# Phase one of a hybrid encoder layer: two buffers for the convolved tile, and the leading products of a block's first feature tile put ahead of those with the tokens' rest

## The chip, the core and the metric

The kernel runs on one core of a Trainium2 chip. The core has five engines with queues of their own: TensorE (PE, with weight loads shown apart as PEld), VectorE (DVE), ScalarE (ACT), GpSimd (POOL) and SyncE (SP, which here issues the DMAs). An engine executes its instructions in the order in which they stand; semaphores make it wait for the others. The metric is the device time of one execution in microseconds (us); 0.3% of it is 8.8 us.

## What is computed

One inference step of one layer for 2048 prompt frames and 32 sample frames of width 1024. The parts of the reference that phase one covers:

```python
h = rmsnorm(x, p['g_mix_pre'])
proj = h @ p['w_in']               # q, k, v (512 each), z (512), xbc (768), dt (8)
xbc_c = silu(causal_dwconv(xbc, conv_prev, w, b))   # 4 taps in time
xh, bm, cm = split(xbc_c)          # 512 + 128 + 128 features
y, h_fin = ssd_scan(xh, dt, a, bm, cm, h0)
y = rmsnorm((y + d_skip * xh) * silu(z), p['g_ssm_out'])
```

After it come stick-breaking attention over q, k, v, the output projection, and a gated feed-forward part with a convolution of width 3, each with its norms and residuals. All inputs and outputs are float32. A float32 product is made of three faster ones: weights and tokens are each split into a leading part (`hi`, type fp32r) and a rest (`lo`), and `hi*hi + hi*lo + lo*hi` is summed in PSUM.

## The kernel before, in words

The 2080 tokens go through phase one in four blocks (`SBS`): three of 512 and one of 544, which carries the sample's 32 and whose groups are cut into two tiles of 272. `phase_in` builds the blocks one after the other (lines 355 to 613), and a scheduler at build time orders the instructions of each engine by their dependencies and estimated lengths, so work of neighbouring blocks is mixed. For a block s:

- `split` (line 314) makes the tokens' leading parts `xhi` on ACT (L319) and the rests `xlo` on DVE (L320), eight 128-feature slices (k-chunks) each. Their pool has one buffer, so a slice can be written only when TensorE has used the same slice of the last block. Block 0 has a form of its own, `first` (L334, L335).
- `dense` (line 158) makes one output tile of 128 features in a PSUM bank named `o`, of which there are two: 24 matmuls, all at L161. For each k-chunk they are `whi*xhi`, `whi*xlo`, `wlo*xhi`.
- Six feature tiles of xbc, in the order 4, 5, 0, 1, 2, 3 (line 371). For each, ACT copies the bank into `raw` (L377), DVE does the first tap (L384) and three more (L388) into `xc`, ACT takes a sigmoid of it (L392), DVE multiplies (L393). `xc` has one buffer. Weights are loaded by SP, split by ACT (L145) and POOL (L146).
- V: eight groups of 24 matmuls of 260 columns (L412), through the same two `o` banks; ACT copies each out into `v` (L421).
- The SSD scan (lines 476 to 565) on DVE, ACT and TensorE, with TensorE filled up by the K and Q groups (L161 again); it works on `xc` in place. Its DMAs (acB, eA) go through SP.
- `prep` (line 295) loads the next block's tokens, sums their squares on ACT (L306) and POOL (L307), and scales them by the root on DVE (L310, eight instructions).
- `gate` (line 616): four groups for z (L161); ACT takes a sigmoid (L627), DVE multiplies with the bank (L628, for block 0 after L625), which sets the bank free, and then `xc` (L630).
- `gate_norm` (line 637): squares (L641, L644, L645), a root (L177, L180, L183), the scaling of `xc` in place (L650), its split on ACT (L654) and POOL (L656, the last readers of `xc`), and the DMAs out (L657, L658).

With one buffer, the next block's first L384 has to come after the last block's L656.

Of the kernel before, what the change touches and what calls it, by code (L numbers as in the profile page):

```python
# [8 lines left out]
F32 = mybir.dt.float32  # L9
# [22 lines left out]
P = 128  # L32
# [33 lines left out]
def tiles_of(n):  # L66
    return [(0, n)] if n <= 512 else [(0, n // 2), (n // 2, n)]


class Kernel:  # L70
# [81 lines left out]
    def parts(self):  # L152
        return tuple([self.xp.tile([P, 544], F32R, name=f"{e}{k}") for k in range(KC)] for e in ("xhi", "xlo"))

    def dense(self, ps, w, x, c0, c1, k0=0, first=True, last=True, pin=False, loose=False):
        nc = self.nc
        xhi, xlo = x
        for k, (whi, wlo) in enumerate(w):
            hi, lo = xhi[k0 + k][:, c0:c1], xlo[k0 + k][:, c0:c1]
            for i, (l, r) in enumerate(((whi, hi), (whi, lo), (wlo, hi))):  # L160
                mm = nc.tensor.matmul(  # L161
                    ps[:, : c1 - c0], l, r,
                    start=first and i == 0 and k == 0,
                    stop=last and i == 2 and k == len(w) - 1,
                    **({"skip_group_check": True} if loose else {}),
                )
                if pin and i == 0 and k == 0:
                    self.pin(mm)
        if pin:
            self.mark(mm)  # L170

# [81 lines left out]
def phase_in(kn, ctx):  # L253
    nc, tc, a, o = kn.nc, kn.tc, kn.a, kn.o
# [60 lines left out]
    def split(s, x):  # L315
        nt = SBS[s][1]
        xhi, xlo = kn.parts()
        for k in range(KC):
            nc.scalar.copy(xhi[k][:, :nt], x[:, k, :nt])  # L319
            nc.vector.tensor_tensor(  # L320
                xlo[k][:, :nt], x[:, k, :nt], xhi[k][:, :nt].bitcast(F32), op=ALU.subtract
            )
        return xhi, xlo

    def first():

        nt = SBS[0][1]
        x = ep.tile([P, KC, 544], F32, name="x")
        xhi, xlo = kn.parts()
        sq = tmp.tile([P, 544], F32, name="sq", bufs=1)  # L330
        for k in range(KC):
            if k % 2 == 0:
                nc.sync.dma_start(x[:, k : k + 2, :nt], a["xT"][:, k : k + 2, :nt])
            nc.scalar.activation(xhi[k][:, :nt], x[:, k, :nt], AF.Copy, scale=kn.col(C_GMIX + k))  # L334
            nc.vector.scalar_tensor_tensor(  # L335
                xlo[k][:, :nt], x[:, k, :nt], kn.col(C_GMIX + k), xhi[k][:, :nt].bitcast(F32),
                op0=ALU.mult, op1=ALU.subtract,
            )
        for k in range(KC):
            if k == 0:  # L340
                nc.scalar.activation(sq[:, :nt], x[:, k, :nt], AF.Square)
            else:
                t = tmp.tile([P, 550], F32, name="t")
                nc.scalar.activation(t[:, :nt], x[:, k, :nt], AF.Square)
                nc.vector.tensor_tensor(sq[:, :nt], sq[:, :nt], t[:, :nt], op=ALU.add)
        return (xhi, xlo), kn.rstd_narrow(rp, psm, "st", [sq], nt, D, tag="r0")
# [8 lines left out]
    for s, (t0, nt) in enumerate(SBS):  # L355
        last = s == NSB - 1
        if s == 0:
            xs, r0 = first()
            rcol = kn.rcol
        else:  # L360
            xs = split(s, nxt)
        xhi, xlo = xs
        raw = ep.tile([P, 6, 550], F32, name="raw")
        xc = kn.xcp.tile([P, 6, 547], F32, name="xc")
        W = 547 if last else 512
        nc.vector.tensor_copy(raw[:, :, 0:3], hist[:])
        if last:
# [3 lines left out]
        for c in (4, 5, 0, 1, 2, 3):  # L371
            w = wfirst if s == 0 and c == 4 else kn.weight(wp, a["wbx"][c])
            for c0, c1 in tiles_of(nt):
                ps = psd.tile([P, 512], F32, name="o")
                kn.dense(ps, w, xs, c0, c1)
                e = min(c1, 512)
                nc.scalar.copy(raw[:, c, 3 + c0 : 3 + e], ps[:, : e - c0])  # L377
                if c1 > 512:
                    nc.scalar.copy(raw[:, c, 518:550], ps[:, e - c0 : c1 - c0])
            if s == 0:  # L380
                nc.vector.tensor_tensor(raw[:, c, 3 : 3 + nt], raw[:, c, 3 : 3 + nt], r0[:, :nt], op=ALU.mult)
            y = xc[:, c, :W]
            wc = C_SW + c * 4
            nc.vector.tensor_scalar(  # L384
                y, raw[:, c, 0:W], kn.col(wc), kn.col(C_SB + c), op0=ALU.mult, op1=ALU.add
            )
            for i in range(1, 4):
                nc.vector.scalar_tensor_tensor(  # L388
                    y, raw[:, c, i : i + W], kn.col(wc + i), y, op0=ALU.mult, op1=ALU.add
                )  # L390
            t = tmp.tile([P, 550], F32, name="t")
            nc.scalar.activation(t[:, :W], y, AF.Sigmoid)  # L392
            nc.vector.tensor_tensor(y, y, t[:, :W], op=ALU.mult)  # L393
# [12 lines left out]
        for b in range(nb):  # L406
            q = min(P, nt - b * P)
            vp = [psd.tile([P, 512], F32, name="o") for _ in range(2)]
            for h in range(2):
                for k in range(KC):  # L410
                    for i, (l, rr) in enumerate(((xhi, wv[0]), (xlo, wv[0]), (xhi, wv[1]))):
                        nc.tensor.matmul(  # L412
                            vp[h][:q, :260], l[k][:, b * P : b * P + q], rr[:, k, h * 260 : h * 260 + 260],
                            start=i == 0 and k == 0, stop=i == 2 and k == KC - 1,
# [40 lines left out]
        ps = psm.tile([P, 512], F32, name="st")  # L455
# [10 lines left out]
        ps = psm.tile([P, 512], F32, name="st")  # L466
# [6 lines left out]
        for b in range(nb):  # L473
# [22 lines left out]
            for g in range(2):  # L496
                rows = slice(g * 64, g * 64 + 64)
                nc.tensor.matmul(cy[:q, g, :q], xc[rows, 4, sl], xc[rows, 5, sl], start=True, stop=True)
                for i in range(2):
# [3 lines left out]
                        start=True, stop=True,  # L503
# [15 lines left out]
            ps = psm.tile([P, 512], F32, name="st")  # L519
# [11 lines left out]
            ps = psm.tile([P, 512], F32, name="st")  # L531
# [16 lines left out]
            ps = psm.tile([P, 512], F32, name="st")  # L548
# [24 lines left out]
        for name, dst in (("wk", kn.kS), ("wq", kn.qS)):  # L573
            for c in range(4):
                w = kn.weight(wp, a[name][c])
                hi = so.tile([P, 544], F32, name="khi")[:].bitcast(F32R)
                lo = so.tile([P, 544], F32, name="klo")[:].bitcast(F32R)
                kf = so.tile([P, 544], F32, name="kf")
                for c0, c1 in tiles_of(nt):
                    ps = psd.tile([P, 512], F32, name="o")  # L580
# [20 lines left out]
        bufs = {"khi": 2, "klo": 2, "t": 2, "sq": 1}  # L601
# [870 lines left out]
def build(nc, tc, a, o):  # L1472
    kn = Kernel(nc, tc, a, o)
    with ExitStack() as ctx:
# [17 lines left out]
        with ExitStack() as c2:  # L1492
            kn.wp, kn.unit, kn.wbufs, kn.rbufs = c2.enter_context(tc.tile_pool(name="weights_in", bufs=1)), KC, 2, 2
            rest = phase_in(kn, c2)
# [125 lines left out]
```

## Time and profile before

| | us |
|---|---|
| median of 3 runs | 2937.35 |
| the runs, lowest to highest | 2936.06 to 2943.05 |
| the profiled execution, its own time | 2941.02 |
| its span in the profile | 2939.2 |
| TensorE busy | 2814.1 (96%) |
| VectorE, ScalarE, GpSimd busy | 1690.8, 1263.4, 1275.4 |

Phase one lies between 0 and about 650 us of the span. In the timeline each row gives the start, the length, the engine, the line and the tiles written and read, `xN` for merged neighbours, and in brackets the time that the engine sat idle before it and what ended that. The waits view sums these idle times by waiting and awaited line: total, times, longest. In the windows view there is, for a stretch, the busy time of an engine and the clock that TensorE was granted (1.00 is full).

### The profile page before, as it was taken

The numbers are of one execution on the slowest core, as the hardware profiler recorded it, in microseconds if no ns is written. First come the engines' busy times: TensorE is split into PE (matmuls) and PEld (weight loads), VectorE is DVE, ScalarE is ACT, GpSimd is POOL, SyncE is SP. The second block draws the span as 40 slices with busy tenths as digits, with TensorE's granted clock in tenths as the row PEclk, the third lists the DMA queues.
The fourth block names the chain that finished last, engine by engine and source line by source line (L and its number), as shares of the span: only waits on it lengthen the run. The fifth ranks groups of instructions, "written<-read, shape, count | busy, mean of one in ns | idle before, by whom it ended". The sixth has DMA issues, their size and how long they took to land.

```text
span 2939.2 us, 46252 instructions
## 1 busy us (share of the span) xinstructions
PE 2814.1 (96%) x16771; PEld 2427.5 (83%) x16771; DVE 1690.8 (58%) x2628; ACT 1263.4 (43%) x2622; POOL 1275.4 (43%) x1131
## 2 busy tenths in 40 slices
PE   7999999989889999999999999999999999999997
PEld 6777777977788888897788888977888889999997
DVE  7667586566773555447555556675666653623333
ACT  4344444337665555446333444654444443321111
POOL 4565555435766666656322323453223233511113
PEclk9999999989999999999999999999999999999999
DMA  5646464648787778777655556656555445765556
GB/s 179 183 137 193 132 176 124 174 115 271 247 282 263 253 263 276 266 256 250 215 180 172 174 180 219 225 182 205 176 172 170 160 159 202 241 181 179 170 178 200
DMA packets 333093, 586.47 MB, mean 200 GB/s; under 512 B 73306, under 2 KB 192738, under 8 KB 332866
## 3 DMA queue, kind: packets, MB, share of 16 engines
q1 hardware_dynamic: 332866, 583.52, 62.1%
q8 instruction: 134, 2.20, 0.3%
q14 instruction: 93, 0.76, 0.1%
HBM read 445.70 MB, written 137.69 MB: 198 GB/s over the span
## 4 chain that ended last, share of the span: by engine, by line
PE 72%; DVE 13%; DMA 7%; ACT 3%; issue 2%; POOL 1%; SPq 1%; DVEq 0%; ACTq 0%; POOLq 0%
PE o L161 35%; PE u L161 12%; PE t L161 10%; PE z L863 4%; PE pa L904 4%; PE pt L882 3%; DVE xc L388 2%; DMA acB<-acD 2%; PE o L412 1%; DVE acB L488 1%; DVE prow L714 1%; DMA xr<-hS 1%; DVE xc L384 1%; DVE xlo L320 1%; DVE x L310 1%
## 5 line engine op out<-in xcount | busy, mean ns | idle before, releaser
L161 PE MATMUL o<-xhi,w 128*128 128x512 f32 (+2 forms) x3968 | 1047.9, 346 | 24.1 <-ACT xhi L334 8.0
L161 PEld LDWEIGHTS o<-xhi,w 128*128 128x128 f32 x3968 | 697.3, 191 | 119.0 <-ACT xhi L334 8.0
L161 PE MATMUL o<-xlo,w 128*128 128x512 f32 (+2 forms) x1984 | 683.8, 345 | 6.3 <-DVE xlo L320 4.2
L146 POOL TENSOR_TENSOR w<-wraw,w 128x512 fp32r<-128x512 f32 (+3 forms) x244 | 384.3, 1577 | 261.4 <-ACT w L145 232.2
L719 POOL TENSOR_TENSOR beta<-beta,prow 128x512 f32<-128x512 f32 (+3 forms) x256 | 252.5, 987 | 442.7 <-DVE prow L714 366.8
L161 PEld LDWEIGHTS o<-xlo,w 128*128 128x128 f32 x1984 | 380.0, 192 | 50.4 <-DVE xlo L320 6.1
L161 PE MATMUL u<-xhi,w 128*128 128x512 f32 x1056 | 350.3, 398 | 0.0
L161 PE MATMUL o<-ah,w 128*128 128x512 f32 x992 | 344.4, 403 | 4.3 <-DVE f L1348 3.8
L1300 POOL TENSOR_TENSOR y<-y,gb 128x512 f32<-128x512 f32 (+1 forms) x88 | 116.0, 1318 | 503.2 <-ACT gb L1299 503.1
L714 DVE TENSOR_TENSOR_SCAN prow<-gam,prow,z 128x513 f32<-128x513 f32 x192 | 245.2, 1278 | 74.1 <-ACT beta L712 69.7
L887 DVE TENSOR_TENSOR wt<-pt,wt 128x512 fp32r<-128x512 f32 (+2 forms) x320 | 191.0, 602 | 159.6 <-ACT wt L886 157.8
L886 ACT CAST wt<-pt 128x512 fp32r<-128x512 f32 (+2 forms) x320 | 166.9, 527 | 218.2 <-PE pt L882 216.3
L145 ACT CAST w<-wraw 128x512 fp32r<-128x512 f32 (+3 forms) x244 | 172.1, 705 | 170.6 <-PE o L161 98.6
L161 PEld LDWEIGHTS u<-xhi,w 128*128 128x128 f32 x1056 | 199.1, 189 | 46.8
L161 PEld LDWEIGHTS o<-ah,w 128*128 128x128 f32 x992 | 187.2, 189 | 47.0 <-DVE f L1348 6.0
L711 ACT ACTIVATE gam<-z 128x512 f32<-128x512 f32 (+2 forms) x320 | 172.3, 538 | 96.0 <-PE z L863 53.9
L161 PE MATMUL u<-xlo,w 128*128 128x512 f32 x528 | 209.5, 397 | 0.0
L161 PE MATMUL o<-al,w 128*128 128x512 f32 x496 | 196.7, 397 | 0.0
L161 PE MATMUL t<-xhi,w 128*128 128x272 f32 x960 | 189.6, 293 | 2.6 <-DMA w<-wS_up 1.7
L882 PE MATMUL pt<-ident,beta 128*128 128x128 f32 x1088 | 180.3, 277 | 4.2 <-DVE wt L887 2.7
L1292 DVE SCALAR_TENSOR_TENSOR y<-gb,cv,y 128x512 f32<-128x512 f32 (+1 forms) x176 | 142.4, 809 | 72.6 <-ACT y L1290 69.9
L904 PE MATMUL pa<-wt,v 128*64 128x256 f32 (+3 forms) x1152 | 172.3, 280 | 8.6 <-DVE wt L887 6.6
(275 smaller groups left out, 4956.4 us busy)
## 6 DMA issues: line engine op xcount, KB each, us to landing
w<-wS_up SPq DMA_DIRECT2D x264, 512.0 KB, 3.6
w<-wS_dn SPq DMA_DIRECT2D x144, 384.0 KB, 3.5
wS_up<-w SPq DMA_DIRECT2D x88, 512.0 KB, 3.4
w<-wS_out SPq DMA_DIRECT2D x78, 512.0 KB, 5.7
wraw<-wup SPq DMA_DIRECT2D x88, 256.0 KB, 4.0
k<-kS SPq DMA_DIRECT2D x80, 256.0 KB, 4.1
v<-vS SPq DMA_DIRECT2D x80, 256.0 KB, 3.8
wS_dn<-w SPq DMA_DIRECT2D x48, 384.0 KB, 3.1
```

The source lines that it names most:

```text
L145: nc.scalar.copy(hi, raw[:, :m, :])
L146: nc.gpsimd.tensor_tensor(lo, raw[:, :m, :], hi.bitcast(F32), op=ALU.subtract)
L161: mm = nc.tensor.matmul(ps[:, : c1 - c0], l, r, start=first and i == 0 and k == 0, stop=last and i == 2 and k == len(w) - 1, **({"skip_gro ...
L711: nc.scalar.activation(g[:, c0:512], z, AF.Sigmoid, scale=-0.125)
L714: nc.vector.tensor_tensor_scan(back(pr), back(g), z[:, 0:1].to_broadcast([P, n + 1]), self.kn.ones[:, 0:1] if prev is None else prev, op0= ...
L719: eng.tensor_tensor(b[:, :n], b[:, :n], pr[:, c0 + 1 : 513], op=ALU.mult)
L863: mm = nc.tensor.matmul(z[:, :n], q[:, P * b : P * b + P], k[:, :n], start=e == 0, stop=e == 1 and kc < s)
L882: mm = nc.tensor.transpose(t[:, P * j : P * j + P], w[:, P * j : P * j + P], kn.ident[:])
L886: nc.scalar.copy(hi, t)
L887: nc.vector.tensor_tensor(lo, t, hi.bitcast(F32), op=ALU.subtract)
L904: nc.tensor.matmul(av[:m, 2 * P * p + c0 : 2 * P * p + 2 * P], v[:, j, :m], wt[:, rest, j, c0:], start=kc == s and p + j + rest == 0, stop ...
L1292: nc.vector.scalar_tensor_tensor(y[:, :W], gb[:, i : i + W], kn.col(wc + i), y[:, :W], op0=ALU.mult, op1=ALU.add)
```

## The change

`xc` gets two buffers. `dense` gets a switch `rests`: with it the 16 products with the leading part of the tokens come first and the 8 with the rests last; it is set for the first feature tile (c == 4) of each block. The sums and their number are the same.

```diff
-    def dense(self, ps, w, x, c0, c1, k0=0, first=True, last=True, pin=False, loose=False):
+    def dense(self, ps, w, x, c0, c1, k0=0, first=True, last=True, pin=False, loose=False, rests=False):
         nc = self.nc
         xhi, xlo = x
+        terms, late = [], []
         for k, (whi, wlo) in enumerate(w):
             hi, lo = xhi[k0 + k][:, c0:c1], xlo[k0 + k][:, c0:c1]
-            for i, (l, r) in enumerate(((whi, hi), (whi, lo), (wlo, hi))):
-                mm = nc.tensor.matmul(
...
+            terms += [(whi, hi), (wlo, hi)] if rests else [(whi, hi), (whi, lo), (wlo, hi)]
+            late += [(whi, lo)] if rests else []
+        for i, (l, r) in enumerate(terms + late):
+            mm = nc.tensor.matmul(
+                ps[:, : c1 - c0], l, r,
+                start=first and i == 0,
+                stop=last and i == 3 * len(w) - 1,
...
-        xc = kn.xcp.tile([P, 6, 547], F32, name="xc")
+        xc = kn.xcp.tile([P, 6, 547], F32, name="xc", bufs=2)
...
-                kn.dense(ps, w, xs, c0, c1)
+                kn.dense(ps, w, xs, c0, c1, rests=c == 4)
```

Every line from 172 of the kernel before on stands three lines lower in the changed one (L384 is L387 there). The scheduler moves other work with it. Three places in the order of instructions:

VectorE, where block 1 follows block 0; `xc_236` is block 0's tile, `xc_1601` block 1's, `t_1638` the sigmoid of block 1's first feature tile, `rstd2` block 0's root. Before:

```order
L320 TENSOR_TENSOR xlo7_1583<-x_1005,xhi7_1575 128x512
L628 TENSOR_TENSOR t_1518<-t_1519,t_1518 128x512
L630 TENSOR_TENSOR xc_236<-xc_236,t_1518 128x512
L183 RECIPROCAL rstd2_1535<-rstd2_1535 128x512
L650 SCALAR_TENSOR_TENSOR xc_236<-xc_236,cv_63,rstd2_1535 128x512 x4
L384 TENSOR_SCALAR xc_1601<-raw_1600,cv_63 128x512 x5
L388 SCALAR_TENSOR_TENSOR xc_1601<-raw_1600,cv_63,xc_1601 128x512 x7
```

The same place in the changed kernel:

```order
L633 TENSOR_TENSOR xc_236<-xc_236,t_1518 128x512
L387 TENSOR_SCALAR xc_1601<-raw_1600,cv_63 128x512
L391 SCALAR_TENSOR_TENSOR xc_1601<-raw_1600,cv_63,xc_1601 128x512 x3
L396 TENSOR_TENSOR xc_1601<-xc_1601,t_1638 128x512
L387 TENSOR_SCALAR xc_1601<-raw_1600,cv_63 128x512
L391 SCALAR_TENSOR_TENSOR xc_1601<-raw_1600,cv_63,xc_1601 128x512 x3
L396 TENSOR_TENSOR xc_1601<-xc_1601,t_1676 128x512
L186 RECIPROCAL rstd2_1535<-rstd2_1535 128x512
L387 TENSOR_SCALAR xc_1601<-raw_1600,cv_63 128x512
L653 SCALAR_TENSOR_TENSOR xc_236<-xc_236,cv_63,rstd2_1535 128x512 x4
L391 SCALAR_TENSOR_TENSOR xc_1601<-raw_1600,cv_63,xc_1601 128x512
```

Two feature tiles of block 1 are now convolved ahead of block 0's root, and the others right behind it.

ScalarE in block 2, where V begins; `t_2978` to `t_3168` are the six sigmoids of the block in order, `o_3173` the first V bank, `o_3174` the second. Before:

```order
L421 COPY v_3223<-o_3173 128x260
L421 COPY v_3223<-o_3174 128x260
L392 ACT_TABLE_LOAD
L392 ACTIVATE t_2978<-xc_2941 128x512
L392 ACTIVATE t_3016<-xc_2941 128x512
L421 COPY v_3283<-o_3233 128x260
L421 COPY v_3283<-o_3234 128x260
L392 ACTIVATE t_3054<-xc_2941 128x512
L392 ACTIVATE t_3092<-xc_2941 128x512
L421 COPY v_3343<-o_3293 128x260
```

The same place in the changed kernel (`o_3100` and `o_3138` are the banks of feature tiles 2 and 3):

```order
L395 ACTIVATE t_3054<-xc_2941 128x512
L395 ACTIVATE t_3092<-xc_2941 128x512
L380 COPY raw_2940<-o_3100 128x512
L145 CAST w_3751<-wraw_3749 128x1024
L395 ACTIVATE t_3130<-xc_2941 128x512
L380 COPY raw_2940<-o_3138 128x512
L145 CAST w_3792<-wraw_3790 128x1024
L424 COPY v_3223<-o_3173 128x260
L395 ACTIVATE t_3168<-xc_2941 128x512
L309 ACTIVATE t_3700<-x_3693 128x544
L309 ACTIVATE t_3703<-x_3693 128x544
L424 COPY v_3223<-o_3174 128x260
```

All six sigmoids stood behind the first two V copies. Five now stand ahead of the first V copy, and three of these (`t_3054`, `t_3092`, `t_3130`) ahead of the copies of feature tiles 2 or 3.

VectorE, where block 2 follows block 1; `t_2758` and `t_2792` belong to the first two gate groups, `x_2353` is block 2's input. Before:

```order
L213 MEMSET rn_v_3727 128x8
L310 SCALAR_TENSOR_TENSOR x_2353<-x_2353,cv_63,rstd_2390 128x512 x8
L628 TENSOR_TENSOR t_2758<-o_2733,t_2758 128x512
L628 TENSOR_TENSOR t_2792<-o_2767,t_2792 128x512
L630 TENSOR_TENSOR xc_1601<-xc_1601,t_2758 128x512
```

The same place in the changed kernel:

```order
L631 TENSOR_TENSOR t_2758<-o_2733,t_2758 128x512
L633 TENSOR_TENSOR xc_1601<-xc_1601,t_2758 128x512
L216 MEMSET rn_v_3727 128x8
L313 SCALAR_TENSOR_TENSOR x_2353<-x_2353,cv_63,rstd_2390 128x512 x8
L631 TENSOR_TENSOR t_2792<-o_2767,t_2792 128x512
```

The first gate product has moved ahead of the eight scalings. On ScalarE the copy of the root that the scalings wait for (L251 there) has moved behind that product's sigmoid and a square that reads its result.

More of the change, by code (lines that the diff above doesn't have):

```diff
@@ L153, in parts @@
         return tuple([self.xp.tile([P, 544], F32R, name=f"{e}{k}") for k in range(KC)] for e in ("xhi", "xlo"))
-    def dense(self, ps, w, x, c0, c1, k0=0, first=True, last=True, pin=False, loose=False):
+    def dense(self, ps, w, x, c0, c1, k0=0, first=True, last=True, pin=False, loose=False, rests=False):
         nc = self.nc
         xhi, xlo = x
+        terms, late = [], []
         for k, (whi, wlo) in enumerate(w):
             hi, lo = xhi[k0 + k][:, c0:c1], xlo[k0 + k][:, c0:c1]
-            for i, (l, r) in enumerate(((whi, hi), (whi, lo), (wlo, hi))):
[L161 to L168, printed above, removed]
+            terms += [(whi, hi), (wlo, hi)] if rests else [(whi, hi), (whi, lo), (wlo, hi)]
[5 more added lines that the diff above has]
+                stop=last and i == 3 * len(w) - 1,
+                **({"skip_group_check": True} if loose else {}),
+            )
+            if pin and i == 0:
+                self.pin(mm)
         if pin:
```

## The prediction

> **What bounds the kernel now.** I read the engines' busy times first, then the windows of 100 us, then TensorE's waits in phase one and their places in the timeline. The first row is from the page; the others are stretches in us with PE's busy share, then all PE busy time (number of matmuls), granted clock, DMA share and GB/s.
>
> ```profile
> PE 2814.1 (96%) x16771; PEld 2427.5 (83%) x16771; DVE 1690.8 (58%) x2628; ACT 1263.4 (43%) x2622; POOL 1275.4 (43%) x1131
> ...
> 600.00:700.00 100.00, 87.68 (x652) 0.91 0.59 179
> 700.00:800.00 100.00, 86.97 (x625) 0.93 0.73 241
> 800.00:900.00 100.00, 92.57 (x628) 0.98 0.80 279
> ```
>
> TensorE is the bound; VectorE, the next, has 58%. Its instructions keep their number, so the change can only fill its idle time or raise its clock. Outside phase one it is idle mainly in 600 to 900: 12.3 + 13.0 + 7.4 = 32.8 us. The waits view of PE from 0 to 660 (total, times, longest) shows what the change can reach:
>
> ```profile
> PE o L412 <- ACT v L421: 8.9, 3, 3.4
> PE o L161 <- DVE t L628: 5.1, 2, 2.6
> PE o L161 <- DVE xlo L320: 4.2, 3, 1.8
> ```
>
> These 18.2 us are the ceiling for waits. The timeline gives their places, each with its idle time in brackets:
>
> ```profile
> 179.34 0.50 PE L161 MATMUL o<-xlo,w 128*128 128x512 f32 x1 [1.63 <-DVE xlo L320]
> 224.95 0.39 PE L412 MATMUL o<-wvhi,xhi 128*128 128x260 f32 x1 [2.88 <-ACT v L421]
> 318.59 0.48 PE L161 MATMUL o<-xhi,w 128*128 128x512 f32 x1 [2.64 <-DVE t L628]
> 337.85 0.50 PE L161 MATMUL o<-xlo,w 128*128 128x512 f32 x1 [1.81 <-DVE xlo L320]
> 386.07 0.39 PE L412 MATMUL o<-wvhi,xhi 128*128 128x260 f32 x1 [3.43 <-ACT v L421]
> 484.04 0.47 PE L161 MATMUL o<-xhi,w 128*128 128x512 f32 x1 [2.48 <-DVE t L628]
> 544.76 0.58 PE L412 MATMUL o<-wvhi,xhi 128*128 128x260 f32 x1 [2.58 <-ACT v L421]
> ```
>
> **The buffer: V's waits.** Here is why ACT copies V late; the first row is from the view of the tile xc (its engine idle in all, times), then ACT and DVE.
>
> ```profile
>   POOL klo L656: 18.4, 3
> ...
> 377.35 1.28 ACT L392 ACT_TABLE_LOAD   x1
> 384.46 1.29 ACT L392 ACTIVATE t<-xc 128x512 f32<-128x512 f32 x2 [5.83 <-DVE xc L388]
> 385.66 0.63 ACT L421 COPY v<-o 128x260 f32<-128x260 f32 x2
> ...
> 207.49 4.44 DVE L384 TENSOR_SCALAR xc<-raw,cv 128x512 f32<-128x512 f32 x5 [5.64 <-POOL klo L656]
> ```
>
> VectorE waits 18.4 us at three boundaries for POOL to read the old `xc`; the convolution comes late; ACT reaches a sigmoid 5.83 us before its input is there, and the V copies queued behind it hold both banks (3.43 us of PE at 386.07). The order of the changed kernel removes it at the root: two feature tiles are convolved ahead of the old block's scaling and the others follow it without a wait for POOL. So the 8.9 us go.
>
> A wait is added in their place: the sigmoids now stand ahead of the raw copies of feature tiles 2 and 3. Behind these copies on ACT stand V's, and PE needs the bank of feature tile 3 when its second V group begins. For block 1, the rows before are:
>
> ```profile
> 193.83 3.35 DVE L183 RECIPROCAL rstd<-rstd 128x512 f32<-128x512 f32 x1 [11.42 <-ACT rstd L180]
> 197.22 4.63 DVE L650 SCALAR_TENSOR_TENSOR xc<-xc,cv,rstd 128x512 f32<-128x512 f32 x4
> ...
> 210.66 0.59 ACT L377 COPY raw<-o 128x512 f32<-128x512 f32 x1 [4.11 <-PE o L161]
> 213.53 0.38 ACT L421 COPY v<-o 128x260 f32<-128x260 f32 x1 [1.33 <-PE o L412]
> ...
> L388 DVE SCALAR_TENSOR_TENSOR xc<-raw,cv,xc x72: 736/744/2920, 42.7 to 542.9; 128x512 f32<-128x512 f32 x54, 128x547 f32<-128x547 f32 x18
> L384 DVE TENSOR_SCALAR xc<-raw,cv x24: 532/540/2645, 38.1 to 534.7; 128x512 f32<-128x512 f32 x18, 128x547 f32<-128x547 f32 x6
> L392 ACT ACTIVATE t<-xc x24: 629/632/667, 51.8 to 543.8; 128x512 f32<-128x512 f32 x18, 128x547 f32<-128x547 f32 x6
> L393 DVE TENSOR_TENSOR xc<-xc,t x24: 678/686/1814, 54.3 to 544.5; 128x512 f32<-128x512 f32 x18, 128x547 f32<-128x547 f32 x6
> ...
> L388 DVE SCALAR_TENSOR_TENSOR xc<-raw,cv,xc 128x512 f32<-128x512 f32 (+1 forms) x72 | 62.8, 922 | 0.0
> L384 DVE TENSOR_SCALAR xc<-raw,cv 128x512 f32<-128x512 f32 (+1 forms) x24 | 24.8, 1075 | 18.4 <-POOL klo L656 18.4
> ```
>
> The last raw copy now stands behind the fifth sigmoid. If the root comes when it did, it ends at 197.2; one first tap (0.54) and the four scalings (4.63) end at 202.4. Then come nine taps of 0.744, two first taps of 0.54 and two products of 0.686 (medians, in ns in the rows): 9.1, to 211.5. The sigmoid (0.63) and the copy (0.59) end at 212.7. The second V group begins when the first is ready to be copied, at 213.5: in time by 0.8. With the means of the last two rows instead (922 and 1075 ns, which hold stretched instructions) nine taps and two first taps take 10.4, with the products 11.8, and the copy ends at 215.4, late by 1.9: the upper end. I take 0.7, nearer to the median's answer of nothing, for each of three blocks: 2.1. V gives **-8.9 + 2.1 = -6.8**; ends -8.9 and -8.9 + 5.7 = -3.2.
>
> **The clock behind these waits.** The windows after three gaps show PE's granted clock (the column behind the number of matmuls):
>
> ```profile
> 318.60:323.00 4.40, 4.40 (x12) 0.61 0.45 146
> 386.10:390.00 3.90, 3.90 (x33) 1.00 0.53 134
> 544.80:549.00 4.20, 4.20 (x22) 0.60 0.79 216
> ```
>
> After the gaps of 2.64 and 2.58 the clock was 0.61 and 0.60, after that of 3.43 it was 1.00. 4.4 x 0.39 and 4.2 x 0.40 are 1.7 us each. I count both as gone with their gaps: **-1.7** here for 544.8, and the other below. [...]
>
> **The gate product, block 1 to 2.** PE's third gate group waited at 318.59 for a bank whose product stood behind eight scalings:
>
> ```profile
> 310.30 7.54 DVE L310 SCALAR_TENSOR_TENSOR x<-x,cv,rstd 128x512 f32<-128x512 f32 x8 [0.45 <-ACT rstd L248]
> 317.77 1.27 DVE L628 TENSOR_TENSOR t<-o,t 128x512 f32<-128x512 f32 x2
> ...
> 311.58 0.60 ACT L627 ACTIVATE t<-o 128x512 f32<-128x512 f32 x1
> 315.99 0.60 ACT L627 ACTIVATE t<-o 128x512 f32<-128x512 f32 x1 [2.87 <-PE o L161]
> ...
> 474.98 8.31 DVE L310 SCALAR_TENSOR_TENSOR x<-x,cv,rstd 128x544 f32<-128x544 f32 x8 [1.55 <-ACT rstd L246]
> ```
>
> The first sigmoid ends at 312.2, so the product (1.27 / 2 = 0.64) can now end at 312.8, before PE wants the bank at 318.59 - 2.64 = 315.95: the gap and its 1.7 of clock go. What is late next is the second product, behind the scalings. These start between 312.8 and some 314.8 (the gate's second product, a square and the root's copy now come ahead, each taken like the 0.6 of these rows), end at 320.3 to 322.3, and the product at 321.0 to 322.9. PE's fourth group wants that bank one group later. The chain of waits has 24 matmuls of L161 in 5.81 us, 0.24 each:
>
> ```profile
> 81.70 5.81 PE o L161 x24
> ```
>
> So it is wanted at 321.8 and the wait is 0 to 1.1; I take 0.7. The boundary 2 to 3, where the product stood ahead of the scalings (474.98) already, still waited 2.48: that is the upper end, and that gap stays.
>
> The place gives **-2.6 - 1.7 + 0.7 = -3.6**; ends -4.3 and -0.1 (2.48 waits, and the clock falls again).
>
> **The leading products first.** They let PE begin earlier, but the group ends when the last rest is written:
>
> ```profile
> 179.81 1.28 DVE L320 TENSOR_TENSOR xlo<-x,xhi 128x512 fp32r<-128x512 f32 x2
> 338.32 1.17 DVE L320 TENSOR_TENSOR xlo<-x,xhi 128x512 fp32r<-128x512 f32 x1
> ```
>
> DVE ends them at 181.1 and 339.5, whatever PE does ahead. Two products stood behind the last rest before, one does now: 0.24 at each of two boundaries, **-0.5**. The wait itself only gathers in front of the rests. Should VectorE write the rests late only because TensorE was late in using the last block's (one buffer), up to 4.2 goes, all of that wait in the view. Block 0 gains nothing: the form `first` has no such wait in the view. Costs of the edit: none by count; the eight rests and the sixteen others are the same matmuls.
>
> **Sum.** -6.8 - 1.7 - 3.6 - 0.5 = -12.6. The profiled execution took 2941.0 (span 2939.2 and 1.8 around it), so 2928.4 on its own time. It lay 3.7 over the median of the runs; the terms are differences inside the span, so on the median 2937.35 - 12.6 = **2924.8 us**.
>
> **The rivals.**
> - The clock falls for a reason of its own: it stayed at 1.00 after the longest gap. Then both 1.7 stay: -9.2, 2928.1. Against it: 0.60 and 0.61 stand right behind two of the gaps.
> - V's wait changes its name: sigmoids ahead of raw copies hold PE as long as sigmoids ahead of V copies did. For it: the margin is only 0.8; against it: the 18.4 us that VectorE no longer waits. What is left is the gate's -3.6 and the -0.5: 2937.35 - 4.1, some 2933.
> - The gain is given back behind phase one. The scheduler's order differs in the attention too, and 600 to 900 has 32.8 us idle, so its waits can grow; if by some 9, more than a quarter: -12.6 + 9 = -3.6, 2933.7. Against it: where windows are full, nothing can be lost.
> - Slower: the convolution becomes the bound of the xbc groups. Each holds PE 5.8 us; a feature tile's chain is 0.54 + 3 x 0.744 + 0.63 + 0.69 = 4.1 by medians and, with 1.075 and 0.922, 5.2 by means. DVE beside a busy POOL stretches taps to 2920 ns (row above). For nine groups (three in each of three blocks) an excess e over 5.8 costs 9e: from e = 1.4, a chain of 7.2, the gain is gone; from 2.4, a chain of 8.2, it is slower by over 0.3%. At e = 3 it is 2937.35 - 12.6 + 27 = some 2952. [...]
>
> That the change does not do what it says is ruled out: the order of instructions shows the convolution ahead of the old scaling.
>
> **How the numbers follow.** The forecast has 0.48, the clock 0.10, V's renamed wait 0.18, the loss behind phase one 0.14, slower 0.10. The low end: -8.9 - 1.7 - 4.3 - 4.2 and some 3.3, a tenth of the 32.8, for luck behind phase one: -22.4, so 2914.9, set down as 2914. The high end takes in the second and third rivals: 2934. A measurement of this kernel can tell about 0.3%, 8.8 us, from no change, so faster is below 2928.5: forecast and clock, 0.58; same: 0.32; slower: 0.10.
>
> **What would show it.** Right: PE's waits on V copies under 2 us in all; those on the gate product some 3 of the 5.1; those on the rests still about 4; no wait of the first tap on POOL; clock 1.00 behind the former gaps. Wrong: PE's V or feature groups waiting for raw copies (second and fourth rival), taps with a mean over 1.2 us, or more than 33 us of idle time in 600 to 900.

## The result, and the profile after

The changed kernel is slower: 2955.49 us median of 4 runs (2952.57 to 2957.53) against 2936.70 for the kernel before in the runs beside it; the ratio is 1.0056, with a 95% interval of 1.0037 to 1.0075, that is 11 to 22 us. Forecast was 12.6 us faster.

The page's row of busy times after:

```profile
PE 2818.3 (95%) x16771; PEld 2433.0 (82%) x16771; DVE 1709.8 (58%) x2628; ACT 1262.0 (43%) x2622; POOL 1276.7 (43%) x1131
```

No engine's share moved by more than a point. Windows of TensorE after (columns as in the prediction), phase one and the stretch in which most of the loss lies:

```profile
0.00:645.00 645.00, 589.00 (x3515) 0.98 0.53 159
...
1290.00:1540.00 250.00, 231.69 (x1335) 0.97 0.65 212
```

The same two in the kernel before:

```profile
0.00:645.00 645.00, 590.90 (x3499) 0.97 0.54 158
...
1290.00:1540.00 250.00, 241.43 (x1364) 0.99 0.67 218
```

Phase one came out even: 56.0 us of idle TensorE against 54.1. Most of the loss is where the prediction did not look: between 1290 and 1540, in the attention with the feed-forward of block 0 woven in, idle time goes from 8.6 to 18.3 us, and the granted clock from 0.99 to 0.97 (some 5 us more over 250, an estimate). A smaller part lies ahead of it. In 700 to 900 the idle time stayed (20.9 us against 20.5), but the clock fell from 0.93 and 0.98 to these:

```profile
700.00:800.00 100.00, 86.08 (x600) 0.90 0.71 233
800.00:900.00 100.00, 93.05 (x615) 0.91 0.77 269
```

That phase one is even does not mean that nothing happened in it. TensorE's waits from 0 to 660 after:

```profile
PE o L415 <- ACT raw L380: 12.2, 5, 4.1
...
PE o L164 <- POOL w L146: 7.0, 10, 1.5
PE o L164 <- ACT raw L382: 3.8, 1, 3.8
PE o L164 <- DVE t L631: 3.0, 2, 2.5
PE o L164 <- ACT raw L380: 2.2, 2, 1.3
...
PE o L415 <- ACT v L424: 1.5, 1, 1.5
PE o L164 <- DVE xlo L323: 0.5, 1, 0.5
```

Before, the waits of the same kinds that the prediction did not show were these:

```profile
PE o L161 <- POOL w L146: 1.9, 3, 1.0
...
PE o L412 <- ACT raw L377: 1.7, 1, 1.7
PE o L161 <- ACT raw L377: 1.4, 1, 1.4
...
PE o L412 <- ACT raw L379: 0.9, 1, 0.9
```

Banks held by V or raw copies cost 8.9 + 1.7 + 1.4 + 0.9 = 12.9 us before and 12.2 + 3.8 + 2.2 + 1.5 = 19.7 after (block 0's own V copies, 3.2 before and 2.0 after, are left out on both sides). Waits for weights rose by 5.1. In return the gate product gave 2.1 and the rests 3.7. The places of the worst new waits, with ScalarE and VectorE ahead of them (timeline of the kernel after):

```profile
190.64 0.63 ACT L395 ACTIVATE t<-xc 128x512 f32<-128x512 f32 x1 [5.39 <-DVE xc L391]
191.17 0.57 ACT L380 COPY raw<-o 128x512 f32<-128x512 f32 x1
191.64 1.05 ACT L145 CAST w<-wraw 128x1024 fp32r<-128x1024 f32 x1
...
223.57 0.63 ACT L395 ACTIVATE t<-xc 128x512 f32<-128x512 f32 x1 [5.21 <-DVE xc L391]
224.11 0.57 ACT L380 COPY raw<-o 128x512 f32<-128x512 f32 x1
...
224.73 0.59 PE L415 MATMUL o<-wvhi,xhi 128*128 128x260 f32 x1 [4.12 <-ACT raw L380]
```

A sigmoid waits 5 us for VectorE's taps; behind it stand the raw copy that frees a bank and the weight cast (L145) on which GpSimd's split of the next weights waits. Why VectorE is late stands in its taps, first as a group from 0 to 700 (busy time, mean ns):

```profile
L391 DVE SCALAR_TENSOR_TENSOR xc<-raw,cv,xc 128x512 f32<-128x512 f32 (+1 forms) x72 | 89.5, 1261 | 1.3
```

The taps' mean went from 0.922 to 1.261 us, their sum from 62.8 to 89.5. Then three of them in the timeline, with GpSimd's row beside them:

```profile
192.49 4.33 DVE L391 SCALAR_TENSOR_TENSOR xc<-raw,cv,xc 128x512 f32<-128x512 f32 x3
...
192.77 2.70 POOL L146 TENSOR_TENSOR w<-wraw,w 128x1024 fp32r<-128x1024 f32 x1 [2.78 <-ACT w L145]
```

The three took 4.33 us, with one GpSimd split of 2.70 us lying within that time. With two buffers the convolution runs earlier, while the weights of the next feature tiles are being split. All 72 taps can be sorted by whether any GpSimd instruction runs beside them. Before, 46 ran with none and 14 beside a weight split; after, 37 and 27. Those with none took 0.75 us on average and 0.79 at most in both kernels; the others averaged 1.22 us before and 1.80 after. So the taps were slow only where GpSimd worked.

### The profile page after: what moved, and what is told of

Same layout as the page of the kernel before. It is cut to its first block, busy times and chain, and to the rows that moved or that the text cites. A ratio compares the mean times of both kernels' runs of the same rounds, so it can differ in the third digit from the quotient of the medians.

```text
span 2955.8 us, 46252 instructions
## 1 busy us (share of the span) xinstructions
PE 2818.3 (95%) x16771; PEld 2433.0 (82%) x16771; DVE 1709.8 (58%) x2628; ACT 1262.0 (43%) x2622; POOL 1276.7 (43%) x1131
## 4 chain that ended last, share of the span: by engine, by line
PE 66%; DVE 4%; DMA 4%; issue 1%; ACT 1%; POOL 1%; SPq 1%; DVEq 0%; POOLq 0%; ACTq 0%
PE o L164 31%; PE u L164 12%; PE t L164 10%; PE z L866 4%; PE pa L907 4%; PE pt L885 3%; DMA xr<-hS 1%; DVE prow L717 1%; DVE xlo L1055 1%; PE u L206 1%; DMA w<-wS_out 0%; PE u L241 0%; DVE f L1383 0%; DMA xhi<-yS 0%; DMA w<-wS_dn 0%
## 5 line engine op out<-in xcount | busy, mean ns | idle before, releaser
L717 DVE TENSOR_TENSOR_SCAN prow<-gam,prow,z 128x513 f32<-128x513 f32 x192 | 245.3, 1278 | 60.1 <-ACT beta L715 56.8
L145 ACT CAST w<-wraw 128x512 fp32r<-128x512 f32 (+3 forms) x244 | 172.1, 706 | 172.2 <-PE o L164 107.6
```

The source lines that it names most:

```text
L145: nc.scalar.copy(hi, raw[:, :m, :])
L717: nc.vector.tensor_tensor_scan(back(pr), back(g), z[:, 0:1].to_broadcast([P, n + 1]), self.kn.ones[:, 0:1] if prev is None else prev, op0= ...
```

## The experiments

Two questions: which stage costs the time, and by what. "Faster" and "slower" below are ratios to the kernel before, in runs on the same chip; 0.1% is 2.9 us.

### Phase one or the order behind it

The scheduler had moved instructions as far as the attention, some 1000 us behind phase one. To part the two, a kernel is built twice: the first build gives an order, the second ties each instruction written after phase one to the one that stood ahead of it on its engine there. This sets the order of issue only, and adds no wait for a result. In the diffs `XC`, `RESTS` and `MARK` are switches: `MARK` is on in the run that bears the name, and off in the build that gives its order.

```diff
+    order = like and program(arrays, like)[1]
...
+            for k in order:
+                if k < late:
+                    continue
+                i = traced[k]
+                e = str(i.engine)
+                if e in prev:
+                    tc.add_manual_dep(
+                        i, prev[e],
+                        mybir.DependencyInfo(mybir.DependencyClass.NoSync, mybir.DependencyReason.DATA),
```

**new_then_old** (phase one of the change, the old order behind it):

> The changed kernel (two xc buffers, leading products first), but every instruction that is written after phase one (attention, output projection, feed-forward, and the last block's gate) stands among its like on all five engines in the order of the kernel before. Theory A (the time is lost in the new order of the attention stage, mostly between 1290 and 1440 us): this is 2935 to 2939 us, no slower than before, since at 745 us the changed kernel was 2 us ahead of the kernel before. Theory B (the time is lost in phase one, by V groups that wait for raw copies, and carried to the end): some 2955 us, as the changed kernel.

**old_then_new** (phase one of before, the new order behind it):

> The kernel before (one xc buffer, no leading products first) in phase one, and behind it the order of the changed kernel on all five engines. Theory A: 2953 to 2957 us, though phase one is that of before, with PE idle over 14 us between 1300 and 1500 instead of 8.6. Theory B: 2935 to 2939 us.

**rests_alone** (the products' order alone):

```diff
-        xc = kn.xcp.tile([P, 6, 547], F32, name="xc", bufs=2)
+        xc = kn.xcp.tile([P, 6, 547], F32, name="xc")
```

> Only the leading products ahead of those with the rests, one xc buffer. Behind phase one the order of instructions stays nearly that of before (DVE differs in 28 rows). If the wait on the rests shrinks from 4.2 to 0.5 us as in the changed kernel by this edit itself: 2932 to 2934 us. If it only gathers in front of the rests, as I predicted: 2936 us, with 3.7 us of PE's waits on xlo left.

**buffer_then_old** (two buffers alone, the old order behind phase one):

```diff
-        xc = kn.xcp.tile([P, 6, 547], F32, name="xc", bufs=2)
+        xc = kn.xcp.tile([P, 6, 547], F32, name="xc", bufs=XC)
...
-                kn.dense(ps, w, xs, c0, c1, rests=c == 4)
+                kn.dense(ps, w, xs, c0, c1, rests=RESTS and c == 4)
```

Here `XC` is 2 and `RESTS` is off.

> Two xc buffers, the old order of products, and behind phase one the order of the kernel before. Against the first kernel of these four it lacks the leading products alone. If the buffer's phase one pays nothing (V's waits renamed to waits on raw copies: about 16.7 us instead of 9.8, against 4.6 of gate waits and 1.7 of clock won): 2936 to 2940 us. If the buffer as such costs (theory B): over 2950.

| kernel | median us | before beside it | ratio, 95% interval |
|---|---|---|---|
| the change | 2955.49 | 2936.70 | 1.0056 (1.0037 to 1.0075) |
| new_then_old | 2944.72 | 2939.71 | 1.0016 (1.0004 to 1.0027) |
| old_then_new | 2952.16 | 2939.71 | 1.0041 (1.0026 to 1.0055) |
| rests_alone | 2939.36 | 2939.71 | 0.9998 (0.9984 to 1.0011) |
| buffer_then_old | 2940.55 | 2939.71 | 1.0005 (0.9993 to 1.0016) |

The two halves add up: 0.16% + 0.41% = 0.57%, and the change costs 0.56%. So about 12 us come from the order behind phase one, with nothing of the edit needed there, and some 5 from phase one (1 to 8 by the interval). Theory A holds for most of the loss; theory B has a small part. TensorE's window agrees, old_then_new first and then new_then_old:

```profile
1290.00:1540.00 250.00, 231.74 (x1330) 0.97 0.65 208
```

```profile
1290.00:1540.00 250.00, 240.80 (x1390) 1.00 0.69 223
```

The place can be narrowed down by taking each VectorE and ScalarE instruction against the same one in the kernel before. The table has the median lag behind it, in us, in three stretches of 100 us (one execution of each kernel):

| kernel | 700 to 800 | 1000 to 1100 | 1600 to 1700 |
|---|---|---|---|
| the change | -1.8 | 3.9 | 16.1 |
| old_then_new | -4.7 | -0.3 | 12.4 |
| new_then_old | 3.9 | 6.5 | 6.5 |
| buffer_then_old | -1.0 | 0.8 | 2.4 |

From the second stretch to the third the new order loses over 12 us, the old one 0 to 1.6. From the first to the second the new order loses 4.4 to 5.7 and the old one 1.8 to 2.6. There the change's clock had fallen; another kernel in the same order (xr4_new_order, below) loses 3.1, so how much of this part belongs to the order stays open.

The products' order alone brings nothing that can be measured; of the 4.2 us of waits on the rests 2.7 stayed.

### What in the new order costs

In the kernel after, at the end of block 0's feed-forward (VectorE, then SyncE's queue, then TensorE):

```profile
1426.93 0.42 DVE L1387 TENSOR_TENSOR f<-f,xr 128x256 f32<-128x256 f32 x1 [6.06 <-DMA xr<-hS]
1427.28 0.68 DVE L1316 TENSOR_TENSOR y<-u,y 128x512 f32<-128x512 f32 x1
1430.63 1.45 DVE L1387 TENSOR_TENSOR f<-f,xr 128x256 f32<-128x256 f32 x1 [2.67 <-DMA xr<-hS]
...
1432.60 1.27 DVE L717 TENSOR_TENSOR_SCAN prow<-gam,prow,z 128x513 f32<-128x513 f32 x1
...
1418.91 0.34 SPq L1388 DMA_DIRECT2D o_yT<-f  x1
1419.30 0.42 SPq L1382 DMA_DIRECT2D xr<-hS  x1
...
1424.14 0.34 SPq L1388 DMA_DIRECT2D o_yT<-f  x1
1424.58 0.54 SPq L1382 DMA_DIRECT2D xr<-hS  x1
...
1428.02 0.60 PE L206 MATMUL u<-ones,fsq 128*128 128x1 f32 x4 [1.38 <-DVE y L1316]
1433.92 0.80 PE L866 MATMUL z<-k,qa 128*128 128x512 f32 x1 [5.30 <-DVE rn_v L223]
```

The residual's addition (L1387) waits 6.06 us for the load of `xr`. That load stands on SyncE's queue behind the store of finished rows (L1388), which itself waits for the addition before. Behind L1387 on VectorE stand the product that frees a bank (L1316) and the scan that frees a score bank (L717), and TensorE waits 1.4, 5.3 and then 2.1 us. The two names in brackets on TensorE are only the last events; the reading is that the time is lost on the loads, and the runs below put it to the test.

**xr4_new_order** and **xr4_old_order** (four buffers for `xr` in place of two, every instruction where it stood):

```diff
-                h = att.tmp.tile([P, 272], F32, name="xr", bufs=2)[:, :n]
+                h = att.tmp.tile([P, 272], F32, name="xr", bufs=4 if MARK else 2)[:, :n]
```

> The changed kernel with every instruction in the place it has there; only the buffers of the residual tile xr in the feed-forward's end go from 2 to 4, so that its loads are issued earlier. Theory E (in the new order VectorE's in-order queue puts additions that wait for xr's load, 16.1 us of waits between 1360 and 1480, ahead of the scans and products that free TensorE's banks; 8.7 us of PE waits between 1428 and 1440): VectorE's waits on xr fall below 5 us there, PE idle in 1290 to 1540 falls from 18 to some 10 us, and the time by 7 to 12 us, to 2944 to 2949. Rival (the other order costs by its matmul sequence, not by xr): the time stays at 2953 to 2957.

> The kernel before, each instruction in its place, with xr's buffers from 2 to 4: the control for the run before this one. VectorE waits 13.5 us for xr's loads there too, but with one PE gap of 3.5 us behind them. Theory E: gain of 2 to 4 us, 2934 to 2937 where before is 2938. If xr's loads cost equally in both orders: the same gain as in the new order.

In the new order 2955.01 us, ratio 1.0058 (1.0043 to 1.0073); in the old 2933.44, 0.9991 (0.9980 to 1.0002). Neither is clear of its counterpart (1.0056, and 1), and VectorE's wait on `xr` in the new order was still 16.1 us. The buffers were not what held the loads: on the queue they still stood behind the stores. So this miss does not test theory E; the next kernel does.

**xr_early_new_order** (four buffers, and block 0's loads moved ahead on SyncE's queue alone):

```diff
+            at = {a: b for a, b in zip(ks[2:], ks[4:])}
+            head = place[kn.stores[0].name]
+            moved = []
+            for k in order[0]:
+                if k == head:
+                    moved += ks[2:4]
+                if k in ks[:2] or k not in ks:
+                    moved.append(k)
+                if k in at:
+                    moved.append(at[k])
...
```

> The changed kernel with every instruction in its place on TensorE, VectorE, ScalarE and GpSimd; on SyncE's queue alone the loads of block 0's residual tile xr stand two places of their own kind further ahead, in front of the stores of the finished rows, with four buffers (the run before this left them behind these stores, and its waits stayed). Theory E: VectorE's waits on xr between 1360 and 1480 fall from 16 to under 6 us, PE's three gaps behind them (1428 to 1440, 8.7 us) to under 3, and the time to 2945 to 2950 on the scale where before is 2938 and the changed kernel 2955. Rival: the gaps stay or are met by another wait, 2952 to 2957.

2946.80 us, ratio 1.0034 (1.0019 to 1.0049). The view of VectorE's waits from 1360 to 1480 and TensorE's window of this run:

```profile
DVE f L1388 <- DMA xr<-hS: 3.4, 3, 1.5
```

```profile
1290.00:1540.00 250.00, 239.23 (x1362) 0.97 0.67 213
```

The wait falls from 16.1 to 3.4 us, TensorE's idle time from 18.3 to 10.8, and the time by some 7 us (1.0058 to 1.0034, with intervals that overlap a little) against the same order with late loads. Of TensorE's three gaps the first is gone, that of 5.3 us is 1.3, and that of 2.1 stays at 2.0. The lag of the table grows by 6.5 us between the second stretch and the third, where the change's grows by 12.2. So the late loads are about half of what the new order costs there. The rest is not parted further; the new order keeps a gap of 3.5 us at a bank that L1352 (L1351 in the change) frees on VectorE behind a scan and four splits (3.96 us).

### What holds phase one

**copies_ahead** (each sigmoid tied behind copies that come later, so that no copy waits for VectorE):

```diff
+            if b == 4 and s and MARK:
+                for sig, n in zip(sigs, (2, 3, 5, 6, 9, 11)):
+                    tc_behind(kn.tc, sig, copies[n])
```

> Two xc buffers, leading products first, behind phase one the order of before, and in blocks 1 to 3 a forced order on ScalarE: each sigmoid of the convolution stands behind raw copies or V copies that come at least 11 us later than its own feature's copy, so no bank is held by a wait for VectorE. The same kernel without this forced order was 0.16% slower than before and had 10.9 + 3.8 + 1.5 us of PE waiting for raw copies. Theory C (sigmoids queued ahead of raw copies hold the banks): these waits fall below 4 us, and the time to 2928 to 2936 us on the scale where before is 2938 (0.1 to 0.3% faster than before). Rival (the convolution on VectorE is itself as long as the matmul groups): the waits go on under other names, 2938 to 2944 us.

2951.65 us, ratio 1.0041 (1.0023 to 1.0058), slower still, and not the gain that theory C forecast. TensorE's waits from 0 to 660 of this run:

```profile
PE y L515 <- DVE xc L405: 14.3, 3, 8.0
...
PE o L429 <- ACT raw L388: 3.1, 1, 3.1
```

The waits on raw copies of V's groups went as expected, from 10.9 to 3.1, and came back as 14.3 us in front of the scan, which needs the last convolved tile (L405 is the product with the sigmoid). But this run does not decide about theory C, since the forced order makes that tile late by itself. In each of the blocks 1 to 3 the last sigmoid starts 11.3 us after its last tap has ended; in new_then_old it starts 0.1 us after. What makes the taps themselves late is tested next.

**weight_rest_by_act** and **weight_rest_by_act_old** (18 of GpSimd's splits taken out, with two buffers and with one; both kernels leave out the true rests of these weights, so that only their times are of use):

```diff
-        nc.gpsimd.tensor_tensor(lo, raw[:, :m, :], hi.bitcast(F32), op=ALU.subtract)
+        if MARK and bx:
+            nc.scalar.copy(lo, raw[:, :m, :])
+        else:
+            nc.gpsimd.tensor_tensor(lo, raw[:, :m, :], hi.bitcast(F32), op=ALU.subtract)
...
-            w = wfirst if s == 0 and c == 4 else kn.weight(wp, a["wbx"][c])
+            w = wfirst if s == 0 and c == 4 else kn.weight(wp, a["wbx"][c], bx=s > 0)
```

> Two xc buffers, leading products first, the order of before behind phase one; every instruction stands where it stood in the run new_then_old, but in blocks 1 to 3 the rests of the six xbc weights are not formed by GpSimd: a ScalarE copy writes a wrong value in their place, so the sums of xbc miss part of their value. It takes 18 GpSimd instructions of about 2.4 us away from beside the convolution's taps and adds 18 of about 1.05 us to ScalarE. Theory D (the taps are stretched by GpSimd's work beside them): the taps' mean falls from 1.26 us to 0.75 to 0.95, PE's waits on raw copies fall by a third or more, PE's waits on weights (8.5 us) mostly go, and the time falls by 5 to 12 us against new_then_old, to 2930 to 2937. Rival (the taps are slow of themselves, or from DMA or ScalarE): mean stays over 1.15 and the time within 3 us of new_then_old.

> The kernel before, one xc buffer and each instruction in its old place, with the edit that gave 29 us in the kernel with two buffers: in blocks 1 to 3 the rests of the xbc weights are written by ScalarE copies of wrong values instead of by GpSimd. Theory D (the second buffer brings the taps beside GpSimd's splits, and so pays only without them): the gain here is clearly smaller than 29 us, some 5 to 15, 2923 to 2933. Rival F (GpSimd's splits cost as much with one buffer): 2908 to 2916, and the buffer brings nothing even where the taps run free.

With two buffers 2915.30 us, ratio 0.9922 (0.9908 to 0.9936), that is 0.94% less than new_then_old; with one buffer 2925.79, 0.9956 (0.9941 to 0.9972). Not a moved instruction lies between each of these and its counterpart, only the engine of 18 of them. The taps as a group from 0 to 700, with two buffers:

```profile
L394 DVE SCALAR_TENSOR_TENSOR xc<-raw,cv,xc 128x512 f32<-128x512 f32 (+1 forms) x72 | 74.6, 1053 | 1.3
```

The three taps shown above, in this run's timeline, and behind them TensorE's waits from 0 to 660:

```profile
184.74 2.33 DVE L394 SCALAR_TENSOR_TENSOR xc<-raw,cv,xc 128x512 f32<-128x512 f32 x3
```

```profile
PE o L167 <- POOL w L149: 4.7, 4, 1.8
PE o L418 <- ACT raw L383: 4.4, 3, 1.8
```

What took 4.33 us beside a split takes 2.33 without it, the waits on raw copies of V's groups fall from 10.9 to 4.4, and those for weights from 8.5 to 4.7. The taps' mean falls to 1.05, not to the 0.75 to 0.95 that I expected (block 0's splits, those of other weights and GpSimd's other work stay), and yet the gain is over twice what I expected. Up to the last tap's end TensorE does the same work in 29 us less, first new_then_old and then weight_rest_by_act:

```profile
0.00:547.00 547.00, 499.99 (x2754) 0.97 0.52 156
...
0.00:518.00 518.00, 485.19 (x2750) 0.99 0.55 165
```

Half of it is idle time (47.0 to 32.8 us); the other half is TensorE's busy time for the same matmuls (500.0 to 485.2), at a granted clock of 0.97 and 0.99, which the expectation had not priced. How much the shorter taps give and how much the weights that are ready earlier is not parted.

Theory D holds, and rival F falls: the same edit is worth 13 us with one buffer and 28 with two. The 13 us do not come through the three taps, whose mean hardly moved (922 to 907 ns). With one buffer the splits lay beside VectorE's other work: the first taps' mean fell from 1075 to 741 ns, that of the scalings (L650) from 1332 to 1008. With GpSimd's 18 splits gone the change's phase one turns from a loss of 0.16% to a gain of 0.34% (0.9922 against 0.9956).

**kept_weights_two_buffers** and **kept_weights_one_buffer** (each xbc weight split once, kept in DRAM, and loaded by the later blocks):

```diff
-            w = wfirst if s == 0 and c == 4 else kn.weight(wp, a["wbx"][c])
+            w = wfirst if s == 0 and c == 4 else kn.weight(wp, a["wbx"][c], key=("bx", c) if MARK else None)
```

> A kernel with the right results that takes GpSimd's splits away: the split xbc weights are written to DRAM when they are first made and loaded by the other blocks (17 of 24 splits go, on ScalarE and GpSimd alike; each such load is 1 MB instead of 0.5 MB); two xc buffers, leading products first, phase one ordered anew by the scheduler, and the order of before behind it. If GpSimd's splits are what stretched the taps: 2912 to 2924. If the larger loads come too late (two weight buffers): PE waits on the weights instead, over 2935.

> The same with one xc buffer and the products in the old order: what the kept weights give without the change. Theory D: 2920 to 2932, at least 5 us behind the kernel with two buffers. Rival F: within 3 us of it.

With two buffers 2931.92 us, ratio 0.9972 (0.9957 to 0.9986), faster than both the kernel before and the change; with one 2938.42, 0.9999 (0.9984 to 1.0013). With two buffers the gain is about a third of that of weight_rest_by_act, for a reason that TensorE's waits (two buffers) show:

```profile
PE o L164 <- DMA w<-wS_bx: 11.0, 7, 3.1
```

The loads are twice as large and TensorE waits 11.0 us for them, the price that the expectation named, though not at its size. With one buffer it waits 15.2 us for them, and the expected gain did not come at all. The two kernels lie 6.5 us apart, in the sense of theory D, but their intervals just overlap. More weight buffers were not tried.

## Why the prediction was wrong, step by step

Two steps failed. The sum has no term for the order behind phase one, which cost some 12 us. And the term for V's waits, -6.8, took the convolution's length from where it stood before: these waits grew by 6.8, and phase one, which was to gain 12.6 us, gained nothing.

- **What bounds the kernel.** Right that only TensorE's idle time and clock could change. Wrong in where: only 600 to 900 was taken as open to loss behind phase one. The full windows around it were read as safe for all that follows, but 1290 to 1540 had 8.6 us idle, and with its new order 18.3. The order showed that rows up to the attention's had moved, and the rival that stood for this was given 9 us and 0.14. It cost 12, of which some 7 on loads of `xr`; the sign set for it, more than 33 us of idle time in 600 to 900, did not come (30.0).
- **The buffer, V's waits (-6.8).** The wait for GpSimd at the boundary did go. But the sum put in its place failed, in the root's time and in "nine taps of 0.744". For block 1 (kernel after):

```profile
199.57 3.35 DVE L186 RECIPROCAL rstd<-rstd 128x512 f32<-128x512 f32 x1 [1.31 <-ACT rstd L183]
...
204.18 3.78 DVE L653 SCALAR_TENSOR_TENSOR xc<-xc,cv,rstd 128x512 f32<-128x512 f32 x4
```

The root ends at 202.9 in place of 197.2: L183 stands behind a sigmoid on ScalarE, and that waited for taps that now come ahead of the root and are stretched. From the scalings' end, 208.0, to the fifth sigmoid, 223.6, it is 15.6 us in place of 9.1. So the last raw copy ends at 224.7 in place of 212.7. The medians were taken from a convolution that mostly ran where GpSimd was idle, and the edit moved it to where GpSimd splits weights. The mean became 1.26, above even the upper end's 0.922. The fourth rival described this mechanism, and priced it on the xbc groups alone. That its 2952 lies near the measured time is chance, since most of the loss arose elsewhere.

- **The new wait on ScalarE.** Right that raw copies would be held; what else stands behind a held sigmoid, the weight cast, was left out. Waits for weights grew by 5.1 us; that all of it comes from held casts is not shown.
- **The clock (-3.4).** Behind the gate's former gap it is 1.00 now (326.1 to 330.5). But the new gaps of 4.12 and 3.79 us have their own slow stretches (the windows after them, kernel after), so nothing was won. Which gaps cost clock in the traces stands in the last section.

```profile
224.80:229.00 4.20, 4.20 (x19) 0.50 0.00 0
...
524.00:528.00 4.00, 4.00 (x18) 0.50 0.02 4
```

- **The gate product (-2.6, +0.7).** Right, nearly to the number: the waits on it fell from 5.1 to 3.0, the fourth group waits 0.55.
- **The leading products first (-0.5).** In waits the other bound was nearer in the changed kernel (4.2 to 0.5). In time the edit alone is worth nothing that can be measured.

## What to carry to other kernels

When an edit lets work start earlier, take its duration from the place it moves to: look at what the other engines do there, and let a median from a quiet place stand only as the lower end. When the order comes from a scheduler, a small edit has two effects, the one that was meant and a new order far behind it; tie the order down to measure them apart before the idea is judged. Four buffers did not bring the loads of `xr` forward while they stood behind waiting stores on SyncE's queue: VectorE's wait stayed at 16.1 us, and fell to 3.4 only with the loads ahead of the stores.

## What the runs showed of the hardware

A VectorE tap with two inputs of 512 columns took 0.75 us on average (0.79 at most) with no GpSimd instruction beside it, and up to 2.9 beside a GpSimd weight split with two inputs of 1024. The mean of the 78 splits between 0 and 700 was 2.43 us before and 2.42 after, while the taps' mean rose from 0.92 to 1.26, so the cost showed on VectorE. The reverse was seen too: in the kernel after, one GpSimd addition of 256 columns took 3.89 us, where the shortest took 0.72 and the median of all 32 of its line is 0.84. VectorE ran eight scalings (3.24 us) and a product behind them in that time:

```profile
1414.45 3.24 DVE L1383 SCALAR_TENSOR_TENSOR f<-f,cv,fsq 128x256 f32<-128x256 f32 x8
...
1415.00 3.89 POOL L1387 TENSOR_TENSOR f<-f,xr 128x256 f32<-128x256 f32 x1 [2.70 <-DVE f L1383]
```

That addition ends at 1418.89, and the store that waits for it is issued at 1418.91: the first link of the 6.06 us wait above. What decides which of the two engines is slowed is not shown.

TensorE's clock was 0.50 after idle times of 4.12 and 3.79 us and 1.00 after 3.13 and 3.43, but 0.60 and 0.61 (half speed for 3.4 us, full for the rest) after 2.58 and 2.64. So the length of a gap does not sort these. In each of the 14 traces all changes of the clock lie on a grid of 3.413 us, and how busy TensorE was within one step of it sorts them better. Kernel before, around the gaps of 2.64 and 3.43 us:

```profile
316.08:319.49 3.41, 0.90 (x4) 1.00 0.54 156
319.49:322.91 3.42, 3.42 (x10) 0.50 0.46 143
380.93:384.34 3.41, 1.71 (x15) 1.00 0.39 77
384.34:387.76 3.42, 1.69 (x14) 1.00 0.20 68
```

The gap of 2.64 us falls almost whole into one step and leaves 0.90 us of work in it, and the next step runs at half speed. That of 3.43 is cut in two by the grid, so that each step keeps half of its work. In the kernels before and after, of the steps at full clock in which TensorE was busy for under 43% of the time, 25 of 25 were followed by half clock; of those over 83%, none of 1,529; between these, 18 of 96. Over all 14 traces it was 195 of 196, none of 10,696, and 116 of 632.
